# First mixer of a two-layer decoder: the masked gram takes the place of z's second buffer

## The chip, the cores and the metric

The kernel runs on one core of a Trainium2 chip. The metric is device time in microseconds (us) from the first to the last instruction of one launch, and what lies around it. Engines named below: PE (TensorE, the matmuls; PEld is its weight load), ACT (ScalarE), DVE (VectorE), POOL (GpSimd), SP (SyncE, which issues most DMAs).

## The reference

Two layers over a sequence of 256 tokens of width 2048, all in float32. Layer 0 mixes with a gated delta rule, layer 1 with sparse attention; both are followed by a layer norm, a convolutional GLU, a second layer norm and a gated projection. Only the first mixer is touched here:

```python
proj = x @ w_in                                  # 256 x 2048 by 2048 x 12352
qkv = silu(causal_dwconv(qkv, conv_w))           # q, k: 16 heads, v: 32 heads, 128 wide
q, k = l2norm(q) * dk ** -0.5, l2norm(k)
lmat = where(strict, (kb @ k.T) * decay, 0.0)    # decay = exp(gc_i - gc_j)
sol = triangular_solve(lmat + I, [vb, kb * exp(gc)])
qk = where(tri, (q @ k.T) * decay, 0.0)
o = ...                                          # from sol, qk and the running state
o = o * rsqrt(mean(o * o) + eps) * norm_g * silu(z)
h = o @ w_o
```

The kernel does the sequence as two halves of 128 tokens rather than as four chunks of 64, which gives the same result: the decay between any two tokens is the exponential of a difference of cumulative gates.

## The kernel before

**Products.** Every large product is done in three passes of a rounded float type: activations and weights are each split into a high part and a rest. ACT writes the high part of a weight tile (`hi`, L116), DVE the rest (`lo`, L117); both have three buffers, and their instructions get a priority ahead of all else. PE multiplies. `gemm_t_steps` computes a product transposed, 256 columns (two tiles of 128) at a time, in four weight tiles; each such block opens two banks of the matmul memory (PSUM), called `mm_ps`. At its end each bank is emptied by `fold` (ACT copies one half out, L226; DVE adds the other, L227). `gemm_steps` computes a product with the tokens on the partitions, one bank for each half of the tokens, called `b_ps`. Both kinds draw from one pool, `self.mm`, of **four** banks. The other four banks are two of tag `sp` and two of tag `bk`.

**Groups.** The mixer works in 8 groups of 4 value heads (2 key heads). In loop turn g (0 to 6) of `gdn_groups` PE does, in program order: `values(g)`, two blocks of 256 columns; `keys(g+1)`, one block for k and one for q of the next group; `zgate(g+1)`, one product of 512 columns whose `done` applies tanh (ACT, L690) and a multiply-add (DVE, L691) into the tile `zs`; then `inverses(g)` and `front(g+1)`. `front` makes the decays, the gram matrix of k (`sums`), the decayed blocks `L`, which go to DRAM as `lt` and come back rearranged as `ld` (`blocks`), and the masked gram `gt`, of which blocks go to DRAM as `lo` (`causal`, L513 to L516). POOL inverts small blocks in `substitute`.

**Interleaving.** `self.inter` is a generator that the products step once at each of their places: three places for a weight tile in `gemm_t_steps`, so 24 in `values` and 24 in `keys`. For group g's solution it holds `finish(g, g+1)`, stepped in turn g+1: `solve` and then `outputs` of group g from the first place, and `mixes(g+1)` from the 25th. `solve` is a chain of small PE products with ACT and DVE steps between them; halfway, the first half's result enters the second (`x_ps`, L704; the update of `v`, L707, DVE) and the second half of v is turned (`v_ps`, L677). `outputs` ends with DVE reading `zs` (tile `ot`, L757). `mixes` multiplies q by k (`gram`, L555 and L556) into two `sp` banks, has DVE multiply them into `qd` and `qo` (L608, L609), and after three more places sums q's squares on PE into another `sp` bank (`ss_ps`, L615). `flush()` after `keys` takes whatever is left.

So `zs` of group g+1 is written at the end of turn g, and read in turn g+2's last part of `keys`: after `zs` of group g+2 has been written.

In turn 7 there is no next group: after `values(7)` the output projection begins (`ahead`), two 512-column products at once, that is, on all four banks of the pool, in six steps that alternate.

**Order.** A planner fixes each engine's order when the kernel is compiled. It goes by priority (program order, less an offset for what is marked as high), takes among the instructions that are ready the first, and counts one that needs a buffer as not ready until a buffer of its tag is free; a tile's buffer is free when all who use the tile have. `self.after(a, b)` forces a behind b in the order of an engine. At run time each engine goes through its own list strictly in order.

**Room.** `gt` shares the one buffer of tag `L` with the decayed blocks, so it can't be written before the DMAs `lt<-L` have read those. Tag `zs` has two buffers; a piece of the input (`xs`) uses it too at the start.

Of the kernel before, what the change touches and what calls it, by code (L numbers as in the profile page):

```python
# [9 lines left out]
F32 = mybir.dt.float32  # L10
# [7 lines left out]
P = 128  # L18
S = 256
# [47 lines left out]
class Trunk:  # L67
# [340 lines left out]
    def gdn(self, ahead):  # L408

        nc, tc, t = self.nc, self.tc, self.t  # L410
        oT = self.oT = self.big.tile([P, 32, 2, S], F32R, tag="big", name="oT")
        with tc.tile_pool(name="gk", bufs=1) as gk, tc.tile_pool(name="gw", bufs=1) as pool:
            cw = gk.tile([P, 4, 64], F32, tag="cw", name="cw")
            ng = gk.tile([P, 1], F32, tag="ng", name="ng")

            xs = [pool.tile([P, 4, S], F32, tag=k, name="x_in", bufs=1 if k == "u" else 2)
                  for k in ("qd", "qd", "zs", "u")]
            w = pool.tile([P, 1024], F32, tag="L", name="gates")
            def load(nb):

                k0 = 4 * nb
                if not nb:
                    src, shape = t["gdn_w_in"], [P, 4, 256]
                    raw = self.wp.tile(shape, F32, tag="raw", name="raw")
                    tiles = [self.hl.tile(shape, F32R, tag=k, name=k) for k in ("hi", "lo")]
                    self.ready[src.tensor.name, src.offset, 0, ((2048, 256),)] = tiles
                for k in (0, 2):
                    nc.sync.dma_start(out=xs[nb][:, k:k + 2], in_=t["x_t"][:, k0 + k:k0 + k + 2])
                    if not nb:
                        nc.sync.dma_start(out=raw[:, k:k + 2], in_=src[k * P:(k + 2) * P, 2048:2304].rearrange(  # L430
                            "(k p) n -> p k n", p=P))
                for k in (0, 2):
                    hi, lo = (self.xT[:, k0 + k:k0 + k + 2, j] for j in range(2))
                    self.halves = self.split(hi, lo, xs[nb][:, k:k + 2])
                    if not nb:
                        self.split(*(x[:, k:k + 2] for x in tiles), raw[:, k:k + 2])
                later = {0: [(w[:, 256 + 32 * i:288 + 32 * i], bass.AP(tensor=t[k].tensor, offset=t[k].offset,
                                                                       ap=[[0, P], [1, 32]]))
                             for i, k in enumerate(("gdn_dt_bias", "gdn_a_log"))],
                         1: [(cw, t["conv_t"]), (self.cst, t["cst"][:, P:C_CMIN]),  # L440
                             (ng, t["gdn_norm_g"].rearrange("(p o) -> p o", o=1)),
                             (self.ident, t["cst"][:, C_IDENT:C_IDENT + P])]}.get(nb, ())
                for out, src in later:
                    self.after(nc.gpsimd.dma_start(out=out, in_=src), self.halves[0], sync=True)
                if nb == 1:
                    nc.gpsimd.tensor_scalar(ng, ng, 0.5, None, op0=ALU.mult)

            self.gdn_groups(pool, gk, cw, ng, oT, load, self.gdn_gates(pool, w, gk), ahead)

    def gdn_groups(self, pool, gk, cw, ng, oT, load, gates, ahead):  # L450
# [4 lines left out]
        nc, t = self.nc, self.t  # L455
# [42 lines left out]
        def causal(s):  # L498

            g, dm = s["g"], s["qd"]  # L500
            do = s["qo"] = pool.tile([P, 4, P], F32, tag="qo", name="qo", bufs=2)
            for h in h4:
                nc.scalar.activation(do[:, h], dm[:, 1, h], AF.Exp, bias=self.gout[:, 4 * g + h:4 * g + h + 1])
            n21 = s["n21"] = pool.tile([P, 4, P], F32, tag="n21", name="n21", bufs=2)
            nc.vector.tensor_tensor(five(n21), bcast(s["gram"][0][:, :, P:S], 2, 2), five(do), op=ALU.mult)
            for a in range(2):
                for h in h4:
                    gc = self.gc[:, a, 4 * g + h:4 * g + h + 1]
                    nc.vector.scalar_tensor_tensor(dm[:, a, h], dm[:, a, h], gc, self.qmin, op0=ALU.subtract, op1=ALU.min)
                nc.scalar.activation(dm[:, a], dm[:, a], AF.Exp)  # L510
            gt = s["gt"] = pool.tile([P, 2, 4, P], F32, tag="L", name="gt")
            for a, ps in enumerate(s["gram"]):
                nc.vector.tensor_tensor(five(gt[:, a]), bcast(ps[:, :, 0:P], 2, 2), five(dm[:, a]), op=ALU.mult)  # L513
            lo = s["lo"] = self.dr.tile([32, 2, 4, 6, 32], F32, tag="lb", name="lo")
            for c in range(3):
                nc.sync.dma_start(out=lo.rearrange("k a h n j -> k (a h) (n j)")[:, :, 32 * pair(c, c + 1):][:, :, :96 - 32 * c],  # L516
                                  in_=gt[32 * c:32 * c + 32, :, :, 32 * c + 32:].rearrange("k a h i -> k (a h) i"))
            sq = s["sq"] = pool.tile([P, 2, S], F32, tag="y0", name="sq")
            nc.scalar.activation(sq, s["q"], AF.Square)
# [31 lines left out]
        def gram(k, y):  # L551
            p1 = self.sp.tile([P, 2, S], F32, tag="sp", name="g1_ps")
            p2 = self.sp.tile([P, 2, P], F32, tag="sp", name="g2_ps")
            for j in range(2):
                nc.tensor.matmul(p1[:, j], k[:, j, 0:P], y[:, j], start=True, stop=True)  # L555
                nc.tensor.matmul(p2[:, j], k[:, j, P:S], y[:, j, P:S], start=True, stop=True)  # L556
            return p1, p2

        def sums(s):
# [43 lines left out]
        def mixes(s):  # L603
            q, k, dm = (s[x] for x in ("q", "k", "qd"))

            p1, p2 = gram(k, q)
            for a, ps in enumerate((p1, p2)):
                nc.vector.tensor_tensor(five(dm[:, a]), bcast(ps[:, :, 0:P], 2, 2), five(dm[:, a]), op=ALU.mult)  # L608
            nc.vector.tensor_tensor(five(s["qo"]), bcast(p1[:, :, P:S], 2, 2), five(s["qo"]), op=ALU.mult)  # L609
            yield from pause(3)  # L610

            pss = self.sp.tile([P, 4], F32, tag="sp", name="ss_ps")
            for h in range(2):
                for a in range(2):
                    nc.tensor.matmul(pss[:, 2 * h + a:][:, 0:1], s["sq"][:, h, a * P:(a + 1) * P],  # L615
                                     self.ones[:, 0:1], start=True, stop=True)
            xm = pool.tile([P, 4, 16], F32, tag="xm", name="xm")
            nc.vector.tensor_tensor(xm, bcast(s["x8"].rearrange("p q e -> p (q e)"), 4, 1), bcast(self.blk, 16, 2),
                                    op=ALU.mult)
            ps8 = self.sp.tile([P, 16, 4], F32, tag="sp", name="s8_ps")  # L620
            nc.tensor.matmul(ps8.rearrange("p e h -> p (e h)"), self.rep, xm.rearrange("p b e -> p (b e)"),
                             start=True, stop=True)
            xh = pool.tile([P, 16, 4], F32, tag="xm", name="xh")
            nc.vector.tensor_tensor(xh, ps8, bcast(self.blk, 16, 1), op=ALU.mult)
            s8 = s["s8"] = pool.tile([P, 4, 2, 2], F32, tag="s8", name="s8", bufs=2)
            nc.vector.tensor_reduce(s8.rearrange("p b q a -> p (b q a)"), xh, axis=mybir.AxisListType.X, op=ALU.add)
            wq = s["wq"] = pool.tile([P, 2, 2], F32, tag="wq", name="wq", bufs=2)
            nc.vector.tensor_scalar(wq.rearrange("p h a -> p (h a)"), pss, 4 * RMS_EPS, RMS_EPS * 128.0,
                                    op0=ALU.add, op1=ALU.mult)
            rr = pool.tile([P, 2, P], F32, tag="y0", name="rr")  # L630
            nc.sync.dma_start(out=rr, in_=bass.AP(tensor=s["rd"].tensor, offset=s["rd"].offset,
                                                  ap=[[0, P], [P, 2], [1, P]]))
            nc.vector.tensor_tensor(five(s["n21"]), bcast(rr, 2, 2), five(s["n21"]), op=ALU.mult)
# [50 lines left out]

        def zgate(s, rest):

            zs = s["zs"] = pool.tile([P, 2, 512], F32, tag="zs", name="zs", bufs=2)

            def done(a, ps):
                nc.scalar.activation(zs[:, a], ps, AF.Tanh, scale=0.5)  # L690
# [83 lines left out]

        def finish(s, n):

            steps = [itertools.chain(solve(s), outputs(s))]
            if n is not None:
                steps.append(itertools.chain(pause(24), mixes(n)))
            while steps:  # L780
                yield
                steps = [x for x in steps if next(x, steps) is not steps]
# [475 lines left out]
```

## Time and profile before

| | |
|---|---|
| median of 3 runs | 2777.17 us (2773.99 to 2779.11) |
| the profiled execution | 2780.57 us |
| its span, first to last instruction | 2778.6 us |
| PE busy | 2738.2 us (99%) |
| DVE, ACT, POOL busy | 1863.4, 1486.4, 349.7 us |
| mean clock granted to PE | 0.998 |
| the mixer's turns 1 to 6 | some 83 to 85 us each, from 135 to 642 us |

Times in the profile are counted from the first instruction. An engine's idle time before an instruction is put down to whatever released it last. A matmul's printed duration overlaps the next one's: eight of L149 in a row take 2.1 us, though one is listed at 0.39 us.

### The profile page before, as it was taken

Reading aid. Unit: us, or ns where it says so; the run is one execution under the profiler, and the core shown is the slowest. Engines: PE = TensorE matmul, PEld = TensorE weight load, DVE = VectorE, ACT = ScalarE, POOL = GpSimd, SP = SyncE. Lnnn points to the kernel's source line nnn. Section 1 sums busy time; section 2 is a strip of 40 time slices with the busy share of each in tenths; the row PEclk is TensorE's granted clock in tenths of the full one; section 3 lists DMA queues with packets and bytes.
Section 4 is the critical chain, followed back from the end, with each engine's and each line's share of the span. In section 5 each row is a group of like instructions: output and inputs, shape, how many; then the busy total and the mean of one; then the engine's idle time right before and its main releaser. Section 6 shows DMA issues by size and latency. Waiting matters only on the chain. (4 is left out here: it accounts for less than half of the span.)

```text
span 2778.6 us, 40034 instructions
## 1 busy us (share of the span) xinstructions
PE 2738.2 (99%) x14604; PEld 2355.0 (85%) x14604; DVE 1863.4 (67%) x3109; ACT 1486.4 (53%) x2512; POOL 349.7 (13%) x682
## 2 busy tenths in 40 slices
PE   8999999999999999999999999999999999999999
PEld 7888888888888888888888889888888888888887
DVE  7878888787556666666545675775676666655566
ACT  5666666666545555555434544455465555543454
POOL 1543334443100000000000000110000000000000
PEclk9999999999999999999999999999999999999999
DMA  7756666666575666766656567555566666665656
GB/s 225 215 150 173 166 186 177 176 173 171 158 238 160 195 203 203 208 196 206 195 193 209 185 179 233 173 149 158 177 188 200 194 191 195 199 194 191 211 170 194
DMA packets 435141, 525.09 MB, mean 189 GB/s; under 512 B 50976, under 2 KB 324496, under 8 KB 434688
## 3 DMA queue, kind: packets, MB, share of 16 engines
q1 hardware_dynamic: 427952, 504.05, 60.4%
q0 software_dynamic: 6992, 18.49, 2.6%
q8 instruction: 115, 1.88, 0.3%
q14 instruction: 82, 0.67, 0.1%
HBM read 516.62 MB, written 8.97 MB: 189 GB/s over the span
## 5 line engine op out<-in xcount | busy, mean ns | idle before, releaser
L117 DVE TENSOR_TENSOR lo<-raw,hi 128x1024 fp32r<-128x1024 f32 (+1 forms) x920 | 1122.3, 1222 | 597.6 <-ACT hi L116 578.4
L116 ACT ACTIVATE hi<-raw 128x1024 fp32r<-128x1024 f32 (+1 forms) x920 | 966.9, 1053 | 698.3 <-PE b_ps L191 416.5
L149 PE MATMUL mm_ps<-xT,hi 128*128 128x512 f32 (+1 forms) x4176 | 1033.6, 395 | 7.7 <-DVE xT L231 5.5
L149 PEld LDWEIGHTS mm_ps<-xT,hi 128*128 128x128 f32 (+1 forms) x4176 | 761.7, 189 | 153.3 <-ACT hi L230 5.5
L153 PE MATMUL mm_ps<-xT,lo 128*128 128x256 f32 (+1 forms) x4176 | 558.5, 285 | 0.4 <-DVE lo L117 0.4
L153 PEld LDWEIGHTS mm_ps<-xT,lo 128*128 128x128 f32 (+1 forms) x4176 | 539.8, 192 | 20.6 <-DVE lo L117 1.2
L188 PE MATMUL b_ps<-hi,xT 128*128 128x512 f32 (+1 forms) x704 | 271.8, 387 | 0.0
L191 PE MATMUL b_ps<-hi,xT 128*128 128x512 f32 (+1 forms) x704 | 268.6, 383 | 0.0
L226 ACT ACTIVATE fold<-mm_ps 128x256 f32<-128x256 f32 x261 | 97.4, 376 | 244.4 <-PE mm_ps L149 244.2
L188 PE MATMUL b_ps<-hi,hTA 128*128 128x512 f32 x512 | 199.2, 389 | 0.0
L191 PE MATMUL b_ps<-hi,hTA 128*128 128x512 f32 x512 | 199.2, 389 | 0.0
L195 PE MATMUL b_ps<-lo,xT 128*128 128x512 f32 (+1 forms) x704 | 187.9, 383 | 0.0
L245 POOL DMA_DIRECT2D lng<-in_ln_g x16 | 8.8, 549 | 1239.1 <-PE b_ps L195 646.9
L644 POOL TENSOR_TENSOR xt<-ld,xi 128x60 f32<-128x60 f32 (+24 forms) x248 | 116.6, 470 | 322.3 <-DMA ld<-lt 303.4
L191 PEld LDWEIGHTS b_ps<-hi,xT 128*128 128x128 f32 x704 | 132.2, 188 | 24.5
L188 PEld LDWEIGHTS b_ps<-hi,xT 128*128 128x128 f32 x704 | 132.1, 188 | 23.9
L195 PEld LDWEIGHTS b_ps<-lo,xT 128*128 128x128 f32 x704 | 130.2, 188 | 24.7
L195 PE MATMUL b_ps<-lo,hTA 128*128 128x512 f32 x512 | 136.8, 389 | 0.0
L646 POOL TENSOR_TENSOR xi<-xi,xt 128x60 f32<-128x60 f32 (+24 forms) x248 | 120.1, 484 | 19.4
L191 PEld LDWEIGHTS b_ps<-hi,hTA 128*128 128x128 f32 x512 | 96.1, 188 | 20.0
L195 PEld LDWEIGHTS b_ps<-lo,hTA 128*128 128x128 f32 x512 | 96.1, 188 | 19.9
L188 PEld LDWEIGHTS b_ps<-hi,hTA 128*128 128x128 f32 x512 | 96.1, 188 | 19.9
(264 smaller groups left out, 2582.4 us busy)
## 6 DMA issues: line engine op xcount, KB each, us to landing
raw<-in_gdn_w_in SPq DMA_DIRECT2D x192, 512.0 KB, 4.7
raw<-in_ffn_w_gate SPq DMA_DIRECT2D x160, 512.0 KB, 4.1
raw<-in_ffn_w_up SPq DMA_DIRECT2D x160, 512.0 KB, 4.2
raw<-in_ffn_w_down SPq DMA_DIRECT2D x160, 512.0 KB, 4.1
raw<-in_dsa_w_in SPq DMA_DIRECT2D x72, 512.0 KB, 3.7
raw<-in_gdn_w_o SPq DMA_DIRECT2D x64, 512.0 KB, 4.3
raw<-in_ple_w_gate SPq DMA_DIRECT2D x64, 512.0 KB, 4.9
raw<-in_dsa_w_o SPq DMA_DIRECT2D x32, 512.0 KB, 4.1
```

The lines of the kernel that those rows point to most:

```text
L116: act = nc.scalar.activation(hi, raw, AF.Copy)
L117: ins = nc.vector.tensor_tensor(lo, raw, hi.bitcast(F32), op=ALU.subtract)
L149: ins = nc.tensor.matmul(q[:m, :], hi[:, k, o:o + m], x[:, k0 + k].rearrange("p a b -> p (a b)"), start=k0 + k == 0, stop=last)
L153: ins = nc.tensor.matmul(q[:m, S:], lo[:, k, o:o + m], x[:, k0 + k, 0, :], start=False, stop=last)
L188: ins = nc.tensor.matmul(ps[a][:, :n], xh, hi, start=k == 0, stop=False)
L191: self.before = nc.tensor.matmul(ps[a][:, :n], xl, hi, start=False, stop=False)
L195: self.last = nc.tensor.matmul(ps[a][:, :n], x(k)[:, 0, a * P:(a + 1) * P], lo, start=False, stop=k == kt - 1)
L226: nc.scalar.activation(t[:m], ps[:, S:], AF.Copy)
L245: ins = self.nc.gpsimd.dma_start(out=r, in_=bass.AP(tensor=src.tensor, offset=src.offset, ap=[[0, P], [1, n]]))
L644: nc.gpsimd.tensor_tensor(tmp[:, :m, :w], bcast(ld[:, i + 1:, i], m, 1), xi[:, :m, i:i + 1].to_broadcast([P, m, w]), op=ALU.mult)
L646: nc.gpsimd.tensor_tensor(xi[:, :m, i + 1:], xi[:, :m, i + 1:], tmp[:, :m, :w], op=ALU.subtract)
```

## The change

`gt` gets a tag and so a buffer of its own. `zs` keeps one buffer, and so does that piece of the input. In `mixes`, q's squares are summed five places after the gram products rather than three, and both the gram products of q with k and the squares' sums are forced behind the last matmul of the weights' product that has been written by then (`self.tail`). In `finish`, group 0's `solve` starts four places later.

```diff
-            xs = [pool.tile([P, 4, S], F32, tag=k, name="x_in", bufs=1 if k == "u" else 2)
+            xs = [pool.tile([P, 4, S], F32, tag=k, name="x_in", bufs=2 if k == "qd" else 1)
...
-            gt = s["gt"] = pool.tile([P, 2, 4, P], F32, tag="L", name="gt")
+            gt = s["gt"] = pool.tile([P, 2, 4, P], F32, tag="gt", name="gt")
...
             for j in range(2):
-                nc.tensor.matmul(p1[:, j], k[:, j, 0:P], y[:, j], start=True, stop=True)
-                nc.tensor.matmul(p2[:, j], k[:, j, P:S], y[:, j, P:S], start=True, stop=True)
+                for ins in (nc.tensor.matmul(p1[:, j], k[:, j, 0:P], y[:, j], start=True, stop=True),
+                            nc.tensor.matmul(p2[:, j], k[:, j, P:S], y[:, j, P:S], start=True, stop=True)):
+                    if y is not k:
+                        self.after(ins, self.tail)
...
-            yield from pause(3)
+            yield from pause(5)
...
-                    nc.tensor.matmul(pss[:, 2 * h + a:][:, 0:1], s["sq"][:, h, a * P:(a + 1) * P],
-                                     self.ones[:, 0:1], start=True, stop=True)
+                    self.after(nc.tensor.matmul(pss[:, 2 * h + a:][:, 0:1], s["sq"][:, h, a * P:(a + 1) * P],
+                                                self.ones[:, 0:1], start=True, stop=True), self.tail)
...
-            zs = s["zs"] = pool.tile([P, 2, 512], F32, tag="zs", name="zs", bufs=2)
+            zs = s["zs"] = pool.tile([P, 2, 512], F32, tag="zs", name="zs")
...
-            steps = [itertools.chain(solve(s), outputs(s))]
+            steps = [itertools.chain(pause(0 if s["g"] else 4), solve(s), outputs(s))]
```

## The prediction

> **What bounds the kernel now.** I read the page first, then the stretch in which the changed code runs, as one row of the view by stages.
>
> ```profile
> span 2778.6 us, 40034 instructions
> PE 2738.2 (99%) x14604; PEld 2355.0 (85%) x14604; DVE 1863.4 (67%) x3109; ACT 1486.4 (53%) x2512; POOL 349.7 (13%) x682
> ```
> ```profile
> 136.00:703.00 567.00, 543.69 (x3109) 472.26 (x3109) 450.86 (x1034) 374.38 (x900) 237.01 (x489) 0.99 0.64 171
> ```
>
> PE sets the end. The change takes no matmul away, so it can win only PE's idle time, and from 136 to 703 us that is 567.0 - 543.7 = 23.3 us. What ended it says the view of PE's waits, with one row of DVE's:
>
> ```profile
> PE v_ps L677 <- DVE v L707: 15.3, 7, 3.4
> PE ss_ps L615 <- DVE qd L608: 5.0, 7, 0.7
> PE y_ps L724 <- DMA pm<-tt: 2.1, 1, 2.1
> ```
> ```profile
> DVE gt L513 <- DMA lt<-L: 22.4, 7, 4.4
> ```
>
> Three rows make 22.4 of the 23.3 us. The fourth is DVE's wait for the room that `gt` shares. The timelines of DVE and of PE in turn 4 show how it reaches PE:
>
> ```profile
> 407.89 1.22 DVE L117 TENSOR_TENSOR lo<-raw,hi 128x1024 fp32r<-128x1024 f32 x1
> 412.70 1.29 DVE L513 TENSOR_TENSOR gt<-g_ps,qd 128x512 f32<-128x512 f32 x2 [3.60 <-DMA lt<-L]
> 414.10 0.68 DVE L707 SCALAR_TENSOR_TENSOR v<-x_ps,v 128x512 f32<-128x512 f32 x1
> ```
> ```profile
> 409.36 1.05 PE L704 MATMUL x_ps<-n,u 128*128 128x128 f32 x8
> 410.17 2.08 PE L149 MATMUL mm_ps<-xT,hi 128*128 128x512 f32 x8
> 414.84 0.66 PE L677 MATMUL v_ps<-ident,v 128*128 128x128 f32 x4 [2.59 <-DVE v L707]
> ```
>
> DVE stands still from 409.1 to 412.7 for the DMA, with the update of `v` queued behind `gt`. Its product was there at 410.4. PE then waits 2.59 us for the turned `v`.
>
> Two of the idle stretches also cost clock. In the stages, and in PE's timeline inside the first of them and just behind it:
>
> ```profile
> 140.00:143.40 3.40, 3.40 (x14) 3.11 (x14) 2.43 (x8) 0.31 (x2) 0.00 (x0) 0.50 0.27 47
> 163.90:167.30 3.40, 3.40 (x16) 3.22 (x16) 2.92 (x5) 2.45 (x8) 2.22 (x4) 0.50 0.69 164
> ```
> ```profile
> 138.77 2.79 PE L153 MATMUL mm_ps<-xT,lo 128*128 128x256 f32 x16
> 141.64 2.93 PE L149 MATMUL mm_ps<-xT,hi 128*128 128x512 f32 x8
> 144.55 2.10 PE L149 MATMUL mm_ps<-xT,hi 128*128 128x512 f32 x8
> 146.85 2.15 PE L153 MATMUL mm_ps<-xT,lo 128*128 128x256 f32 x16
> ```
>
> The granted clock is 0.50 for 3.4 us after the wait of 2.1 us for `pm`, and again after the longest for `v` (3.4 us). The same work takes 2.93 - 2.10 = 0.83 and 2.79 - 2.15 = 0.64 us more: 1.5 us for each stretch, 3.0 for both.
>
> **The change, part by part.** *gt on its own:* in turns 1 to 7 nothing of `gt` waits for `lt<-L` any more. In turn 4 DVE could do `gt` at 409.1 to 410.4 and the update of `v` by 411.1, while PE's eight matmuls last until 412.2. What is late next is ACT's copy of the turned `v`, as far behind it as before. Gain: between 0 (the order is planned anew) and 15.3, and I take 14. No instruction is added, and its three DMAs `lo<-gt` only start earlier.
>
> *Squares two places later:* the sums need a bank that DVE's L608 frees 0.7 us late. Two places are about a weight tile's matmuls less one place, over 2 us. Gain 5.0; 0 if the product of q with k moves with it. `wq`, which they feed, is read only in the next turn's outputs.
>
> *Group 0's solution four places later:* the DMA into `pm` lands 2.1 us after PE asks; four places are longer. Gain 2.1. The clock's 3.0 us go with these waits, and I count 2.4 of them. *The ties* cost nothing where the products stand behind those matmuls already, as they do in turn 4; they only forbid filling a hole with them.
>
> Sum of gains: 14 + 5.0 + 2.1 + 2.4 = 23.5 us.
>
> *z's second buffer:* this is the price. The views of ACT and DVE, turn 3's end and turn 4's end:
>
> ```profile
> 388.71 0.60 ACT L690 ACTIVATE zs<-b_ps 128x512 f32<-128x512 f32 x1 [1.21 <-PE b_ps L195]
> 390.58 0.58 ACT L690 ACTIVATE zs<-b_ps 128x512 f32<-128x512 f32 x1
> ```
> ```profile
> 449.06 0.86 DVE L757 SCALAR_TENSOR_TENSOR ot<-o_ps,rs,zs 128x128 f32<-128x128 f32 x3
> 450.97 1.38 DVE L757 SCALAR_TENSOR_TENSOR ot<-o_ps,rs,zs 128x128 f32<-128x128 f32 x5
> 454.45 0.41 DVE L227 TENSOR_TENSOR pd<-mm_ps,fold 128x256 f32<-128x256 f32 x1
> ```
>
> At 388.7 the gate of group 4 is written into one buffer, while that of group 3 lies in the other until L757 has read it at 452.4. With one buffer, group 4's tanh can't start before 452.4. Until then its product stays where PE put it: in two of the four banks, for 62 of a turn's 84 us. `values` and `keys` have two banks instead of four, and each block of 256 columns must wait for the folds of the block before it. That happens in turns 1 to 6 at four places each, and in turn 7. What such a place costs is not in the trace, since every block now starts on the other two banks. The bounds come from the folds at the end of turn 4's first block, by PE, ACT and DVE:
>
> ```profile
> 401.83 2.10 PE L149 MATMUL mm_ps<-xT,hi 128*128 128x512 f32 x8
> 403.77 0.83 PE L717 MATMUL l_ps<-ys,LB 128*128 128x128 f32 x6
> ```
> ```profile
> 403.74 0.38 ACT L226 ACTIVATE fold<-mm_ps 128x256 f32<-128x256 f32 x1 [0.21 <-PE mm_ps L149]
> 405.37 0.37 ACT L226 ACTIVATE fold<-mm_ps 128x256 f32<-128x256 f32 x1
> ```
> ```profile
> 404.15 0.42 DVE L227 TENSOR_TENSOR pd<-mm_ps,fold 128x256 f32<-128x256 f32 x1 [0.59 <-ACT fold L226]
> 406.64 0.41 DVE L227 TENSOR_TENSOR pd<-mm_ps,fold 128x256 f32<-128x256 f32 x1
> ```
>
> The block ends at 403.7. The first bank is free at 404.6, 0.9 us later, the second at 407.1, 3.4 us later, as weight splits come between. Low bound 0.9, less what PE has to do there anyway; high bound 3.4. In between PE can do the first tile's matmuls alone, if they are planned so, hence nearer the low bound: I add 0.6, a quarter of the 2.5 us between the banks.
> - values to values: the six `l_ps` cover 0.6 us. 0.3 + 0.6 = 0.9.
> - values to k: no small matmul follows directly. 0.9 + 0.6 = 1.5.
> - k to q: eight `o_ps` of about 0.9 us follow (row below), so 0 + 0.6 = 0.6.
> - q to z: q's block ends at 451.2, where z's next product begins (second row below). DVE is at L757 until 452.4; a fold's add right behind it frees a bank at 452.8, 1.5 us later. In the order of before that add ends at 454.9, 3.6 us later. I take 1.8, near the low end, since the planner has then a reason to put it first.
>
> ```profile
> 437.29 1.05 PE L744 MATMUL o_ps<-u,qd 128*128 128x128 f32 x8
> 451.15 0.39 PE L188 MATMUL b_ps<-hi,xT 128*128 128x512 f32 x1
> ```
>
> A turn pays 0.9 + 1.5 + 0.6 + 1.8 = 4.8 us, six turns 28.8 (bounds: 0.3 + 0.9 + 0 + 1.5 = 2.7, six times 16; 2.8 + 3.4 + 2.5 + 3.6 = 12.3, six times 74).
>
> *Turn 7* wants all four banks for the output projection and gets two until group 6's `ot` is done:
>
> ```profile
> 673.07 0.39 PE L188 MATMUL b_ps<-hi,oT 128*128 128x512 f32 x1
> 677.75 0.48 PE L188 MATMUL b_ps<-hi,oT 128*128 128x512 f32 x1
> ```
> ```profile
> 702.48 0.86 DVE L757 SCALAR_TENSOR_TENSOR ot<-o_ps,rs,zs 128x128 f32<-128x128 f32 x3
> ```
>
> The second product (677.75) would stand still, and its weights hold the three `hi` buffers after the first product's third step. The solution's chain, freed of the products between its steps, ends sooner than 703.3. I count 2.5 us (bounds 0 and 10).
>
> Sum: -23.5 + 28.8 + 2.5 = +7.8 us. The profiled execution (2780.57 us, span plus 2.0) lies 3.4 us above the median; the sum is a difference, and I set it on the median: 2777.2 + 7.8 = 2785.
>
> **A rule beside this.** The Trainium skill, "TensorE: Matmul & The Clock Gate", section "A second HAM failure mode: psum-queue depth-cycling", says that small idles between groups of matmuls as PSUM banks are cycled can make the clock gate swing between half and full. Its section "Part 1: The HAM clock gate" puts the idle window before half clock at some 3.4 us. Here a wait of 2.1 us was followed by half clock, so this trace has it trip sooner, if not each time (two low stretches, against seven waits for `v`). The first section speaks against the change, and is the third rival below.
>
> **The rivals.**
> 1. *The banks hardly cost.* The planner fills the holes with small matmuls and first-tile matmuls, and DVE, freed of 22.4 us of standing still, folds at once. Then the low bound of 16 us, less another 4 for holes filled, and 0 in turn 7: -23.5 + 12 = -11.5, 2766. For it speaks that PE waits for no fold anywhere in the waits quoted; against it, that no block has to now.
> 2. *Even.* The low bound as it stands, with turn 7: -23.5 + 16 + 5 = -2.5, 2775.
> 3. *The clock.* Beside the forecast's loss, the q-to-z wait trips the clock gate in each of six turns and turn 7 twice: 8 x 1.5 = 12 us more, 2797.
> 4. *The second bank decides.* The order was planned with other durations, so that PE asks for the second tile before its late fold, everywhere: 74 instead of 28.8, and 10 in turn 7: 2777 - 23.5 + 84 = 2838. For it speaks that L227's second add came 2.5 us behind the first; against it, that the planner knows of the bank's want. It decides if a place costs over some 2 us on the mean.
> 5. *The waits only move.* `v` is late for another reason, as DVE is 80% busy here (450.9 of 567.0): the gain is 9.5 instead of 23.5, the loss as forecast: 2799.
>
> **How the numbers follow.** Forecast 0.34, rival 1 0.27, rival 2 0.17, rival 3 0.07, rival 4 0.06, rival 5 0.09. A measurement of this kernel can tell some 0.2%, 5.6 us, from no change. Rival 1 lies beyond it but for its upper edge (0.26 faster), with 0.05 from the lower edges of rival 2 and the forecast: faster 0.31. Same: the rest of rival 2, 0.13, and the forecast's lower part, 0.12: 0.25. Slower: 0.44. The forecast's own range is 2778 to 2797. Eight in ten reach from 2759 (all of the gains, 25.4 us, and 7 us for the banks) to 2812 (23.5 us gained, and 58 lost, some 9 us in a turn).
>
> **What would show it.** In the waits: `gt <- lt` gone; `v_ps <- v` near nothing; `ss_ps` gone; `y_ps <- pm` gone. New rows: `mm_ps L149` or `L153` waiting for DVE's L227, some 18 times, and `b_ps L188` waiting for L227 or L691. L690 of group 4 stands not behind its product but after L757, more than 50 us later. PE's idle time in this stretch would rise from 23 to some 30 us. I am wrong if mm_ps waits for no fold, if L690 is still within 2 us of its product, or if the clock falls to 0.50 in many places.

## The result and the profile after

The changed kernel is slower. Its median is 2818.78 us (2813.56 to 2820.34, 4 runs), against 2778.14 us (2773.99 to 2780.08, 4 runs) of the kernel before: ratio 1.0145, 95% interval 1.0127 to 1.0163, some 40 us. The profiled execution took 2820.34 us; its mean clock is 0.990 instead of 0.998. From here on line numbers of the changed kernel are two higher than before from L558 on: L706 is the product `x_ps` and L709 the update of `v` behind it, L617 the squares' sums, L692 and L693 the tanh and multiply-add into `zs`, L726 the product with `pm`, L759 `ot`, L765 the transposes of `ot`.

The first two lines of the page of the changed kernel:

```profile
span 2817.5 us, 40020 instructions
PE 2758.7 (98%) x14604; PEld 2367.3 (84%) x14604; DVE 1861.5 (66%) x3109; ACT 1485.9 (53%) x2512; POOL 329.8 (12%) x682
```

The span grew by 38.9 us. PE's idle time went from 2778.6 - 2738.2 = 40.4 to 58.8 us, 18.4 more, and its busy time from 2738.2 to 2758.7, 20.5 more, with the same 14604 matmuls. So half of the loss is waiting, and half is PE being busy for longer over the same matmuls.

Where it lies is seen if the mixer is cut at DVE's updates of `v`, one in each turn (start of one to start of the next, us):

| stretch | before | after | after with two `zs` buffers (x9 below) |
|---|---|---|---|
| start to the first update | 162.0 | 157.5 | 159.4 |
| turns 1 to 6 | 504.2 | 527.7 | 478.5 |
| turn 7 | 67.9 | 87.7 | 68.0 |
| the rest of the span | 2044.4 | 2044.6 | 2044.1 |

The view by stages for turn 4 and turn 7, first of the changed kernel, then of the kernel before (start and end, length, then busy time and instructions of PE, PEld, DVE, ACT, POOL, then PE's clock, the DMA share and GB/s):

```profile
421.60:510.00 88.40, 85.09 (x468) 73.26 (x467) 67.81 (x155) 56.65 (x135) 31.33 (x71) 0.96 0.65 167
685.20:772.90 87.70, 71.65 (x355) 59.48 (x354) 42.21 (x74) 41.23 (x95) 28.59 (x70) 0.90 0.49 147
```
```profile
414.10:499.00 84.90, 80.98 (x466) 70.39 (x466) 67.66 (x155) 56.67 (x135) 34.65 (x71) 1.00 0.65 173
666.30:734.20 67.90, 66.49 (x347) 56.02 (x348) 42.24 (x77) 40.18 (x94) 33.44 (x70) 1.00 0.59 174
```

In turn 4 PE's idle time is lower, if anything (3.3 instead of 3.9 us); it is busy 4.1 us longer at a clock of 0.96. In turn 7 idle time went from 1.4 to 16.1 us.

PE's waits after, and one row each of ACT's and DVE's:

```profile
PE ot_ps L765 <- DVE ot L759: 17.9, 12, 5.3
PE y_ps L726 <- DMA pm<-tt: 10.2, 1, 10.2
PE ss_ps L617 <- DVE qd L610: 5.5, 5, 1.2
PE mm_ps L149 <- DVE pd L227: 0.9, 3, 0.4
```
```profile
ACT L L495 <- DMA qd<-grow: 21.8, 7, 4.6
```
```profile
DVE qd L509 <- ACT L L495: 13.6, 7, 3.2
```

The waits for `v` (15.3 us before) and of `gt` (22.4 us) are gone. In their place stand the transposes of `ot`, which did not wait before; one long wait for `pm`; and the squares' sums, which were to lose theirs. PE waits for a fold three times, 0.9 us together.

The end of turn 4's block for q, in the timelines of DVE, ACT and PE:

```profile
458.77 0.35 DVE L509 SCALAR_TENSOR_TENSOR qd<-qd,gc,cst 128x128 f32<-128x128 f32 x1 [1.66 <-ACT L L495]
463.03 1.38 DVE L759 SCALAR_TENSOR_TENSOR ot<-o_ps,rs,zs 128x128 f32<-128x128 f32 x5
464.60 0.42 DVE L227 TENSOR_TENSOR pd<-mm_ps,fold 128x256 f32<-128x256 f32 x1 [0.20 <-ACT fold L226]
```
```profile
465.42 1.06 ACT L692 ACTIVATE zs<-b_ps 128x512 f32<-128x512 f32 x2
```
```profile
400.08 0.62 PE L195 MATMUL b_ps<-lo,xT 128*128 128x512 f32 x2
...
459.84 2.00 PE L149 MATMUL mm_ps<-xT,hi 128*128 128x512 f32 x8
463.43 0.66 PE L765 MATMUL ot_ps<-ident,ot 128*128 128x128 f32 x4 [1.59 <-DVE ot L759]
463.92 0.38 PE L679 MATMUL v_ps<-ident,v 128*128 128x128 f32 x2
464.46 0.55 PE L765 MATMUL ot_ps<-ident,ot 128*128 128x128 f32 x3 [0.16 <-DVE ot L759]
465.08 0.58 PE L188 MATMUL b_ps<-hi,xT 128*128 128x512 f32 x1
```

z's product for group 4 is done at 400.7, and its tanh runs at 465.4, right behind `ot` (until 464.4): the product lay in its two banks for 65 us. The next one (L188) starts at 465.08, 3.24 us after the block before it, q's, ended at 461.84; the transposes and `v_ps` fill some 1.4 of these, and PE is idle for 1.8. It starts 0.05 us after DVE has freed the first of q's two banks: that fold's add (L227) stands right behind `ot` and ends at 465.03. In turns 2, 3, 5 and 6 it is the same. The 0.58 us of that matmul, where 0.39 was usual, show a lower clock. The view by stages has it at half in three places of turns 4 and 7: behind the squares' wait of turn 4, behind the wait just shown, and in turn 7:

```profile
441.50:444.90 3.40, 3.40 (x17) 3.21 (x15) 1.54 (x3) 1.40 (x3) 2.77 (x9) 0.50 0.76 142
465.40:468.80 3.40, 3.40 (x9) 2.67 (x8) 3.40 (x7) 3.40 (x9) 0.00 (x0) 0.50 0.79 193
714.50:731.60 17.10, 6.56 (x20) 5.00 (x21) 3.97 (x10) 3.67 (x10) 7.86 (x21) 0.50 0.08 15
```

Between 50 and 2700 us the clock records of the changed kernel have ten such stretches, 51.2 us in all, against two and 6.8 us before. If half of PE's busy time in them is lost (an estimate), eight of 3.4 us cost 1.7 each, one of 6.8 us (195.7 to 202.5, PE busy for 4.3) costs 2.2, and the long one 6.56 / 2 = 3.3: 19.1 us together, less 3.4 before, or some 16 of the 20.5 us of added busy time. The other 5 I can't assign.

Turn 7 in PE's timeline, with the projection's matmul that comes behind the wait:

```profile
709.04 0.60 PE L679 MATMUL v_ps<-ident,v 128*128 128x128 f32 x4
714.89 2.15 PE L765 MATMUL ot_ps<-ident,ot 128*128 128x128 f32 x8 [5.25 <-DVE ot L759]
727.19 0.77 PE L726 MATMUL y_ps<-vs,pm 128*128 128x128 f32 x2 [10.15 <-DMA pm<-tt]
727.61 0.77 PE L188 MATMUL b_ps<-hi,oT 128*128 128x512 f32 x1
```

In the kernel before, the products of the output projection ran without a gap at this place and the product with `pm` came behind them. Here PE's order has group 7's product with `pm` ahead of the second projection product, which had no banks, and PE waits 10.15 us for the DMA. The DMA is not late: POOL issues it from 723.3 us on, 38 us into the turn, and in the kernel before from 709.1 us on, 43 us into it. It is the product that comes early.

### The profile page after: what moved, and what is told of

Same layout as the page of the kernel before. It is cut to its first block, busy times and chain, and to the rows that moved or that the text cites. A ratio compares the mean times of both kernels' runs of the same rounds, so it can differ in the third digit from the quotient of the medians.

```text
span 2817.5 us, 40020 instructions
## 1 busy us (share of the span) xinstructions
PE 2758.7 (98%) x14604; PEld 2367.3 (84%) x14604; DVE 1861.5 (66%) x3109; ACT 1485.9 (53%) x2512; POOL 329.8 (12%) x682
## 5 line engine op out<-in xcount | busy, mean ns | idle before, releaser
L188 PE MATMUL b_ps<-hi,xT 128*128 128x512 f32 (+1 forms) x704 | 274.9, 392 | 0.4
L191 PE MATMUL b_ps<-hi,xT 128*128 128x512 f32 (+1 forms) x704 | 271.2, 387 | 0.0
L188 PE MATMUL b_ps<-hi,hTA 128*128 128x512 f32 x512 | 199.2, 389 | 0.0
L188 PEld LDWEIGHTS b_ps<-hi,xT 128*128 128x128 f32 x704 | 133.8, 190 | 26.9 <-DVE pd L227 1.6
L188 PEld LDWEIGHTS b_ps<-hi,hTA 128*128 128x128 f32 x512 | 96.1, 188 | 19.9
L648 POOL TENSOR_TENSOR xi<-xi,xt 128x60 f32<-128x60 f32 (+24 forms) x248 | 102.3, 412 | 19.4
```

The source lines that it names most:

```text
L188: ins = nc.tensor.matmul(ps[a][:, :n], xh, hi, start=k == 0, stop=False)
L191: self.before = nc.tensor.matmul(ps[a][:, :n], xl, hi, start=False, stop=False)
L648: nc.gpsimd.tensor_tensor(xi[:, :m, i + 1:], xi[:, :m, i + 1:], tmp[:, :m, :w], op=ALU.subtract)
```

## The experiments

Each is timed against the kernel before on the same chip; the number is the ratio, with its 95% interval. Letters of theories are those of the quoted expectations. The kernel before was timed anew in each of four sets of runs, with medians of 2778.1 (the change), 2785.0 (x1, x2, x3, x5), 2788.8 (x6, x7, x9, x10) and 2786.3 us (x4, x11, x12, x13); in the later three its executions had mean clocks of 0.993 to 0.999. The change itself was timed in the first set alone. A difference between ratios of two sets can therefore be some 0.4%, 10 us, off, and where that matters the medians, or the spans of the profiled executions, stand beside it.

| run | edit | ratio | median, us |
|---|---|---|---|
| (the change) | | 1.0145 [1.0127, 1.0163] | 2818.8 |
| x1_z1 | before, one `zs` buffer | 1.0154 [1.0129, 1.0180] | 2828.2 |
| x10_gtown | before, `gt` on its own | 0.9884 [0.9870, 0.9899] | 2755.5 |
| x9_all2 | after, two `zs` buffers | **0.9872** [0.9857, 0.9886] | 2752.1 |
| x11_scratch | before, control for the room | 1.0001 [0.9987, 1.0014] | 2786.9 |
| x4_noties | after, no ties | 1.0057 [1.0041, 1.0073] | 2802.0 |
| x12_z7 | after, own `zs` for group 7 | 1.0079 [1.0060, 1.0099] | 2807.1 |
| x5_turn7 | after, projection in other steps | 1.0106 [1.0078, 1.0134] | 2815.6 |
| x13_fill | after, matmuls added into a wait | 1.0080 [1.0060, 1.0099] | 2808.5 |
| x6_pause8 | after, squares still later | 1.0111 [1.0095, 1.0126] | 2818.8 |
| x7_ottie | after, `ot`'s transposes tied behind z's matmuls | 1.0143 [1.0126, 1.0160] | 2827.1 |
| x3_gt, x2_z2 | `gt` in `ld`'s buffer | 1.0421, 1.0426 | 2902.2, 2903.4 |

**z's buffer alone (x1_z1).**

```diff
-            xs = [pool.tile([P, 4, S], F32, tag=k, name="x_in", bufs=1 if k == "u" else 2)
+            xs = [pool.tile([P, 4, S], F32, tag=k, name="x_in", bufs=2 if k == "qd" else 1)
...
-            zs = s["zs"] = pool.tile([P, 2, 512], F32, tag="zs", name="zs", bufs=2)
+            zs = s["zs"] = pool.tile([P, 2, 512], F32, tag="zs", name="zs")
```

> The kernel before, with one buffer for zs and nothing else of the change. Theory A (z's product held in two of four banks is the whole loss, with the half clock that follows its waits): slower than the change itself, 2820 to 2850 us, since the gains for v, pm and the sums are missing; no L690 within 50 us of its product. Theory B (the ties and the later places make the loss, the banks little, as in the prediction's first rival): 2772 to 2788 us.

Measured 1.0154, 43 us, from this edit alone: theory B falls. It is not slower than the change by more than the intervals, as theory A had it. PE's waits:

```profile
PE v_ps L677 <- DVE v L707: 25.0, 7, 4.6
PE ot_ps L763 <- DVE ot L757: 14.8, 12, 4.6
PE y_ps L724 <- DMA pm<-tt: 11.8, 2, 9.2
```

The waits for `ot` and `pm` come with the buffer, and the one for `v`, which `gt` causes, stays and grows. So the buffer alone costs as much as the whole change loses. In the profiled execution the start and turns 1 to 6 take 29.8 us more than before, and turn 7 takes 21.2 more (89.1 instead of 67.9 us).

**`gt` without its price: two misses (x3_gt, x2_z2).** To give `gt` a place and keep both `zs` buffers, it shared `ld`'s buffer, in the kernel before (x3_gt, shown) and in the changed one with the lines for `xs` and `zs` as before (x2_z2):

```diff
-            gt = s["gt"] = pool.tile([P, 2, 4, P], F32, tag="L", name="gt")
+            gt = s["gt"] = pool.tile([P, 2, 4, P], F32, tag="ld", name="gt")
```

> The kernel before, with gt in the one buffer of ld in place of L's; zs keeps two. Theory A: gt no longer waits for lt, v_ps waits go (15.3 us and 1.5 us of half clock), nothing is lost: 2760 to 2767 us. Rival C (v is late for another reason, the wait only moves): 2774 to 2781 us, with v_ps still waiting over 10 us.

> The whole change, but with two buffers for zs, and gt in the buffer of ld. Theory A: all of the gains and none of the loss, 2752 to 2763 us. Theory B: the ties and later places still cost, 2790 us or more.

Both 4% slower, for a reason of their own (DVE's and PE's waits of x3_gt):

```profile
DVE gt L513 <- POOL xt L644: 128.8, 8, 19.2
```
```profile
PE g_ps L555 <- DVE gt L513: 128.6, 8, 18.3
```

The buffer went to `ld` first, so `gt` waited until POOL's inversion had read it. They say nothing on the theories.

**The same with real room (x10_gtown, x9_all2, x11_scratch).** The 4 KB per partition came from the memory for DMA descriptors. x10_gtown is before with `gt` on its own; x9_all2 is the whole change with two `zs` buffers; x11_scratch is before with less descriptor memory and nothing else.

```diff
-            gt = s["gt"] = pool.tile([P, 2, 4, P], F32, tag="L", name="gt")
+            gt = s["gt"] = pool.tile([P, 2, 4, P], F32, tag="gt", name="gt")
...
-    nc = bacc.Bacc("TRN2", target_bir_lowering=False, num_devices=1, dynamic_dma_scratch_size=8192)
+    nc = bacc.Bacc("TRN2", target_bir_lowering=False, num_devices=1, dynamic_dma_scratch_size=4096)
```

That is x10_gtown. x11_scratch has the last two lines alone; x9_all2 has them in the changed kernel, with the lines for `xs` and `zs` as they were before.

> The kernel before, with gt in a buffer of its own and zs still in two; the room comes from half of the memory set aside for the descriptors of DMAs (8192 to 4096 bytes). Theory A: gt waits neither for lt nor for POOL, PE's 15.3 us for v and some 1.5 us of half clock go and nothing is lost: ratio to before 0.993 to 0.995 (2762 to 2767 us where before is 2781). Rival C (the wait for v moves to another cause): 0.998 to 1.001. Against both: the smaller descriptor memory holds POOL's DMAs up, over 1.001, and pm or ld land later.

> The whole change but with two buffers for zs, room as in x10. Theory A (the held product is the whole loss): all gains and no loss, ratio 0.990 to 0.993. Theory B (ties and later places cost by themselves): above 1.000.

> The kernel before, with half the memory for the descriptors of DMAs and nothing else: the control of the runs that take their room from there. Theory A: no change, ratio 0.998 to 1.002. Rival: the smaller memory is itself a part of their gain, 0.990 to 0.996.

The room costs nothing (1.0001). `gt`'s buffer alone brings 1.16%, 32 us, and the whole change with two buffers 1.28%, 36 us (2752.07 us, median of 4); both are more than theory A forecast. This version beats both kernels. Its turn 4, and PE's waits:

```profile
397.20:477.50 80.30, 80.30 (x468) 70.44 (x467) 67.38 (x156) 56.42 (x135) 32.60 (x71) 1.00 0.69 182
```
```profile
PE y_ps L726 <- DMA pm<-tt: 1.0, 1, 1.0
PE v_ps L679 <- DVE v L709: 0.5, 1, 0.5
PE ss_ps L617 <- DVE qd L610: 0.5, 1, 0.5
```

PE is busy for all 80.30 us. Set on the same scale, the single `zs` buffer costs 1.0145 - 0.9872 = 2.73%, 76 us, in company with the other parts (67 us between the two medians), and 1.54% alone.

**The ties (x4_noties).** The changed kernel without both ties:

```diff
-                    if y is not k:
-                        self.after(ins, self.tail)
+                    pass
...
-                    self.after(nc.tensor.matmul(pss[:, 2 * h + a:][:, 0:1], s["sq"][:, h, a * P:(a + 1) * P],
-                                                self.ones[:, 0:1], start=True, stop=True), self.tail)
+                    nc.tensor.matmul(pss[:, 2 * h + a:][:, 0:1], s["sq"][:, h, a * P:(a + 1) * P],
+                                     self.ones[:, 0:1], start=True, stop=True)
```

> The changed kernel without the two ties to the weights' product. If the ties mend what the held banks do to the order: products of q with k or sums stand earlier, with longer waits for ss_ps, ratio 1.0155 to 1.02. If they do nothing: 1.0125 to 1.0155, the same order on PE but for a few products.

I had the ties at nothing, or at a help, in every theory. Without them the kernel is at 1.0057: with one `zs` buffer they cost 0.88%, some 24 us (17 between the medians, and between the spans), 18.6 of it in turns 1 to 6 (509.1 instead of 527.7 us). PE's timelines of turn 4 show what they hold back, without the ties (where lines are one lower) and with them:

```profile
423.42 0.39 PE L556 MATMUL g_ps<-q,k 128*128 128x128 f32 x2
...
432.88 0.95 PE L616 MATMUL ss_ps<-cst,sq 128*128 128x1 f32 x8
```
```profile
431.75 0.59 PE L555 MATMUL g_ps<-q,k 128*128 128x256 f32 x2
...
439.96 1.02 PE L617 MATMUL ss_ps<-cst,sq 128*128 128x1 f32 x8 [1.15 <-DVE qd L610]
```

Without them the planner had put the products of q with k 9.5 us ahead of the sums and DVE was done in time. Tied, they come at one place together, 8.2 us ahead of the sums, and DVE's L610, between other work, ends late. The wait for the sums is gone in x4_noties (it has no such row), and the clock's half stretches fall from 51.2 to 37.5 us. In x9_all2, which has the ties, the sums wait 0.5 us in all, and that version is no slower than x10_gtown, which has none: with two `zs` buffers the ties cost little. That they cost where the order is short of other matmuls is my reading; no run varies that alone.

**The squares still later (x6_pause8).**

```diff
-            yield from pause(5)
+            yield from pause(8)
```

> The changed kernel, with the squares' sums eight places after the gram products rather than five. Theory E (a wait of 1.2 us before the sums also trips half clock for 3.4 us in each turn): the wait of five turns goes, 5.5 us, and the half clock behind it, 1.5 us each: ratio to before 1.008 to 1.011. Rival F (the clock stretches come from elsewhere): only the wait goes, 1.012 to 1.0135, and the half clock about 76 us after the one behind the ot waits stays.

The squares' wait goes, and the half clock falls to 34.1 us, but seven waits for a fold come in its place:

```profile
PE mm_ps L149 <- DVE pd L227: 6.6, 7, 1.5
```

PE's idle time between 100 and 820 us rose from 43.0 to 47.5 us. By the ratio, 1.0111, the kernel got faster; its median is that of the change, 2818.8 us, and the interval reaches what F forecast. This run decides nothing between E and F.

**Work added into a wait (x13_fill).** Ahead of the first transposes of `ot` in turns 1 to 6, seven matmuls of 512 columns go into the bank that the transposes then overwrite. They add 42 matmuls, and change nothing of the output.

```diff
+                    for k in range(7 if g < 6 and not a else 0):
+                        nc.tensor.matmul(ps.rearrange("p h t -> p (h t)"), self.xT[:, k, 0, 0:P],
+                                         self.xT[:, k].rearrange("p a b -> p (a b)"), start=True, stop=True)
```

> The changed kernel with seven matmuls of 512 columns more (0.23 us each) in front of the first transposes of ot in turns 1 to 6, into the bank that the transposes overwrite: work added where PE waits. Theory E (idle PE is what trips half clock): the stretches behind the ot waits go, 1.5 us for each, and the added work lies in the wait: ratio 1.009 to 1.0135. Rival F (the clock falls for another reason): 1.6 us more in each of six turns, 1.0145 to 1.018, and the stretches stay.

1.0080: with more work the kernel is 0.65% faster, some 18 us (10 between the medians, 16 between the spans). The ratio is below theory E's range; with 10 us it would be inside. PE's timeline at the end of turn 4, where the wait had been (the transposes are L768 there):

```profile
452.16 1.78 PE L765 MATMUL ot_ps<-xT 128*128 128x512 f32 x7
453.78 1.08 PE L768 MATMUL ot_ps<-ident,ot 128*128 128x128 f32 x8
454.69 0.60 PE L679 MATMUL v_ps<-ident,v 128*128 128x128 f32 x4
455.13 0.60 PE L555 MATMUL g_ps<-k 128*128 128x256 f32 x2
457.15 0.51 PE L188 MATMUL b_ps<-hi,xT 128*128 128x512 f32 x1 [1.42 <-DVE zs L693]
```

Of the half clock, 23.9 us in two stretches are left, neither of them in turns 2 to 6; by the estimate above they cost 4.1 us instead of 19.1. F falls, since it had the kernel slower and the stretches still there, and E is borne out: waits of one or two microseconds cost about as much again by the clock. The planner also laid other work differently here (the squares' wait fell to 0.9 us), so not all of the gain need be the clock.

**What the next z product waits for (x7_ottie).** In the changed kernel the holes are labelled `ot`. Is it `ot`, or the bank? Tied behind the last of z's matmuls that has been written by then, the transposes stand elsewhere:

```diff
                         if not h:
                             self.after(t, ins, sync=True)
+                        if g < 6:
+                            self.after(t, self.last)
```

> The changed kernel, with the transposes of ot forced behind z's matmuls of the place where they are written (turns 1 to 6). Theory G (PE would have to wait there anyway, for q's folds to free banks; the transposes only stand in that hole): the row ot_ps waiting for ot nearly goes, b_ps of L188 waits for L227 instead, 1.5 to 3 us six times, and the time is within 6 us of the changed kernel, 1.012 to 1.0165. Rival H (the transposes are put too early, and that is the cost): 1.0105 or less, and no new wait for L227.

The time stays (1.0143; the median is 8 us above the change's), and the label moves. PE's waits and its timeline at the end of turn 4:

```profile
PE b_ps L188 <- DVE zs L693: 16.8, 4, 4.5
PE ot_ps L765 <- DVE ot L759: 5.5, 1, 5.5
PE b_ps L188 <- DVE pd L227: 2.3, 1, 2.3
```
```profile
469.07 0.50 PE L188 MATMUL b_ps<-hi,xT 128*128 128x512 f32 x1 [3.66 <-DVE zs L693]
```

Here PE's order asks first, in turns 3 to 6, for a bank that z's old product holds, and `b_ps` waits for the gate's last read of it; in turn 2 it waits for q's fold, as the changed kernel does. So the hole belongs to the banks, and `ot_ps` only stood in it. Theory G was right in this, though it named the fold alone. Either bank comes free only behind `ot`.

**Turn 7 (x5_turn7, x12_z7).** x5_turn7 does six steps of the first projection product alone, and then six of the second. x12_z7 gives group 7's `zs` a buffer of its own, so that its product needs not wait for group 6's `ot`.

```diff
-                ahead(3, ())
+                ahead(6, (), (0,))
...
-                ahead(3, rest)
+                ahead(6, rest, (1,))
...
-        def ahead(n, rest):
+        def ahead(n, rest, which=(0, 1)):
...
-                for g in begun:
+                for g in [begun[i] for i in which]:
```
```diff
-            zs = s["zs"] = pool.tile([P, 2, 512], F32, tag="zs", name="zs")
+            zs = s["zs"] = pool.tile([P, 2, 512], F32, tag="z7" if s["g"] == 7 else "zs", name="zs")
```

The second, x12_z7, has the smaller descriptor memory too.

> The changed kernel, with the output projection's two products of turn 7 one after the other: six steps of the first, then six of the second. Theory A (in turn 7 the second product's want of banks leaves PE idle, and the order has PE wait for pm instead): turn 7 loses its waits of 5 and 10 us and most of its half clock, 2800 to 2806 us. Rival D (pm is late in itself in turn 7, whatever stands before it): the 10 us wait for pm stays, 2813 to 2820 us.

> The changed kernel, with a buffer of its own for the zs of group 7 alone (room as in x11): turns 1 to 6 still hold a product in two banks, turn 7 does not. Theory A: turn 7's share, some 20 us, goes: ratio 1.006 to 1.009. Rival D (pm's late landing is turn 7's cost whatever the banks do): 1.0125 to 1.015, with the wait of 8 to 10 us for pm still there.

With its own buffer turn 7 takes 73.7 us instead of 87.7 and the kernel 1.0079, as theory A forecast: 14.0 us of turn 7, or 0.66%, some 18 us, by the ratio. The wait for `pm` falls to 3.9 us, so rival D falls. Other steps alone bring little (83.6 us; 1.0106, which the change's own interval overlaps), against theory A's forecast, since the second product has no banks yet and the wait for `pm` stays:

```profile
PE y_ps L726 <- DMA pm<-tt: 8.2, 1, 8.2
```

## Why the prediction was right in its sign and wrong in its size

The sign was right, 1.45% slower; the time, 2819 us, lies outside the range of 2759 to 2812. Of the signs of being wrong that it listed, one came true: the clock fell to 0.50 in ten places.

**The mechanism held.** z's product is kept in two of the four banks for 65 us ("more than 50 us later"), its tanh comes right behind `ot`, and the next z product, left with q's two banks, waits for a fold right behind `ot`, as the step q to z had it: PE is idle for 1.8 us in turn 4, as estimated. Rival 5 (waits only move) falls: with two buffers the waits for `v` are gone. Rival 4 (the second bank) falls: the waits put down to folds are 0.9 us in all.

**Where the miss lies.** The spans of the profiled executions, all read against the one that the prediction used, allow a sum by terms; each is a single execution, and those of one kernel lie 7 us apart here (2813.6 to 2820.3 us). Up to turn 7 the change without its ties (x4_noties) takes 1.4 us more than before, where the forecast had 28.8 - 23.5 = 5.3. The ties add 17.5 us to that, where it had nothing. Turn 7 takes 19.8 us more, where it had 2.5. These three make 38.7 of the 38.9 us. The step that failed outright is thus **"the ties cost nothing"**, and the term that was mis-sized most is turn 7.

**The gains were too small: 23.5 predicted, 36 measured** (0.9872; 32 to 40 us), or 28.5 between the spans. The idle time was sized rightly: from 136 to 703 us it falls from 23.3 to 1.9 us, as this row of x9_all2 shows:

```profile
136.00:703.00 567.00, 565.08 (x3250) 493.41 (x3250) 462.33 (x1052) 389.03 (x930) 229.07 (x497) 1.00 0.68 180
```

The term that was mis-sized is the clock, 2.4 us. The profiled execution had two half stretches; most other executions of before have a lower mean clock (0.993 to 0.999) than its 0.998, where x9_all2's has 1.000 in all four. x11_scratch's profile, the same program but for the room, has five, each 0.7 to 1.5 us after the start of an update of `v`; its span is 31.6 us longer than x9_all2's, 10.5 of it PE's busy time. Its PE timeline and stage:

```profile
416.07 1.11 PE L677 MATMUL v_ps<-ident,v 128*128 128x128 f32 x4 [3.16 <-DVE v L707]
```
```profile
416.00:419.40 3.40, 3.33 (x12) 2.94 (x13) 3.18 (x8) 1.55 (x5) 1.04 (x2) 0.50 0.68 139
```

**The single buffer's price was much too small: 31.3 predicted, 43 measured alone (51 between the spans) and 76 with the rest (67).** The 28.8 us for turns 1 to 6 come near the 29.8 of x1_z1 by luck: half of the time that these turns gained there, 15.9 of 31.1 us, is PE being busy for longer, at a clock of 0.97. Step by step:
- *Values to values, to k, and k to q* (3.0 us a turn, 18 in all) cost 0.9 us in waits for a fold. The planner put first-tile matmuls and small ones there; on this one point rival 1 was right.
- *Turn 7* (2.5 us, bounds 0 and 10) cost 19.8 us: I had the second product stand still, and had not asked what the order would put in its place. It was the product with `pm`, whose DMA PE then waits for 10.2 us, behind 5.3 us for `ot`, and at half clock besides.
- *The clock* was left out of the forecast and is the steady turns' largest part: turn 4 is 3.5 us longer than before with less idle time. Rival 3 named it and gave it 12 us and a chance of 0.07; the estimate above comes to some 16 more than before.
- *The squares' sums* were to win 5.0 us and wait 5.5 us, because of the ties. I read from turn 4 of before that the products stood behind those matmuls already, in an order that was about to be planned anew with two banks fewer.

With the two effects measured alone, 0.9872 x 1.0154 = 1.0024, 7 us slower: near the forecast's +7.8, by two errors that cancel (12 us of missing gain, 12 of missing price). The other 33 us come where the parts meet; by the spans it is 38.9 - (51.0 - 28.5) = 16.4 us, about what the ties add. Which part of that is the clock can't be told, since x4_noties, x12_z7 and x13_fill overlap.

**Still open:** why `ot` itself is later than before, ending 2.6 us behind q's block in turn 4 instead of 1.0. DVE waits 13.6 us for ACT's L495, which waits 21.8 us for the DMA of `grow` (7.6 before, 7.8 in x9_all2). That wait comes with the single buffer and not with the ties (20.1 us in x1_z1, 21.2 in x4_noties). Whether it is a cause, or follows from products that come late, no run tells.

## What to carry to other kernels

A single buffer on the SBUF side is paid where its next contents wait: before giving one up, look up when its next write would start and its last read ends, and count as held whatever source (here half of a PSUM pool) sits between them. Forced orders that cost little with two buffers cost most of a per cent here with one, so try each with and without the rest of the change. Count each short wait of PE twice when the clock can fall behind it, and before trading one buffer for another, look for room outside the tiles, as the descriptor memory was here.

## What the runs showed of the hardware

Waits far shorter than a stretch of half clock can start one: one of 1.15 us behind six small and ahead of eight one-column matmuls did (turn 4, 439.96 us), while 2.59 us did not in turn 4 of before (412.25 to 414.84 us). The half stretches last 3.413 us, or whole multiples, on one fixed grid (worked out from the clock records); x11_scratch's five begin at 160.0, 245.4, 330.7, 416.0 and 501.4 us, 25 grid steps of 3.413 us apart, in turns of 85.0 to 86.1 us. So a loop whose turn is near a multiple of the grid meets it in the same phase each time; that may be why one execution of a program has two such stretches and another five, though no run was made to show it. The grid of before, counted from its stretch at 140.0 us, has a step at 413.1 us, which splits the 2.59 us into 0.8 and 1.8; in x11_scratch 3.1 of the 3.16 us ahead of 416.07 lie in a single step. That fits, but it is worked out afterwards from two cases.

The Trainium skill, "TensorE: Matmul & The Clock Gate", section "Part 1: The HAM clock gate", has the clock decided over free-running windows of 4096 cycles, some 3.4 us, and half clock after an idle window. The grid agrees; an idle window was not needed here, as the 1.15 us show. Its section "A second HAM failure mode: psum-queue depth-cycling" tells of another kernel, in which short idles between groups of matmuls, as PSUM banks are cycled, make the clock swing between half and full. x13_fill agrees: with the hole that the bank leaves filled, the half clock fell from 51.2 to 23.9 us.
